# Experts' weights loaded as one consecutive run a partition: a two-layer mixture-of-experts and hybrid mixer kernel

## The chip, the cores and the metric

The kernel is one program on one core of a Trainium2 chip. The metric is the device time of one execution in microseconds (us), as the median of several runs. The core has TensorE (PE; its weight loads are listed apart as PEld), VectorE (DVE), ScalarE (ACT), GpSimd (POOL) and SyncE (SP), which here issues most of the DMAs. All inputs lie in HBM, and all arithmetic data are 32 bits wide.

## What is computed

Two blocks stand one behind the other, each of two layers, for 256 tokens of width 1024 (and 256 context tokens in the first layer). What the change touches is the mixture of experts at the end of each layer of the first block:

```python
D_MODEL = 1024; N_EXPERTS = 32; TOP_K = 2; D_EXPERT = 512; MOE_BLOCK = 128

def hier_moe(h, w_rg, b_rg, w_re, b_re, w1, w3, w2):
    ...                      # a group of 8 experts, then 2 experts of it, for each token
    xs = h[slot_tok].reshape(n_blocks, MOE_BLOCK, d_)
    def run(args):
        xb, e = args
        return (jax.nn.silu(xb @ w1[e]) * (xb @ w3[e])) @ w2[e]
    ys = lax.map(run, (xs, block_e)).reshape(-1, d_)
    return jnp.zeros_like(h).at[slot_tok].add(ys * slot_gate[:, None])
```

`w1` and `w3` of an expert are 1024 x 512 matrices, `w2` is 512 x 1024; each is 2 MB. Layer 0 runs it on 512 tokens (256 of `x` and 256 of `ctx`), layer 1 on 256. Before it, in each layer, stand a modulation, a dense input product, attention, local mixers and a dense output product; behind both layers stands the second block (sliding window and forgetting attention, a state space mixer, memory attention), which has no experts.

## The kernel before

**The stream of weights.** All large weights pass through `Stream`. A unit is a tile `wu` of 128 partitions by 2048 numbers, 1 MB. Units are pushed in the order in which they will be used; `pump` gives the next one a free slot and issues its DMA on SP's queue, where it waits until the last reader of the slot's former content is done. There are some 13 or 14 slots during the experts. `push_kn` (L188) loads the dense weights, `push_ex` (L203) the experts' weights. An expert's number stands in a register that SP reads from the routing result.

**The experts.** The 32 experts are ranked by their load. A plan fixed when the kernel is built gives each rank a capacity of 128 tokens (the first ones; one has 256 in layer 1), 64 or 32, and packs them into groups of 128 rows: one expert of 128 ("b"), two of 64 ("m") or four of 32 ("s"). Blocks of two to four groups are worked through in three stages: A (product with `w1`, silu), B (product with `w3`, multiply), C (transpose of the result, product with `w2`, scatter). A stage of a group takes two halves of the depth, and each half needs one unit of each of the group's experts: two units for a "b" stage, four for "m", eight for "s". A layer has 32 experts of 6 units, 192 units, of which 128 are `w1` or `w3` and 64 are `w2`.

**What a partition of a unit holds.** In `push_ex` the rows of the matrix are split as `(k p)`: partition p holds row k * 128 + p for each k. A unit of `w1` or `w3` has four such rows of 512 numbers (k = 0 to 3), one of `w2` two rows of 1024. So a partition is filled by four runs of 2 KB, or by two of 4 KB.

**What multiplies them.** The rows of a unit are the depth of a product, so the other operand must have its depth on the same partitions. For stages A and B this is `xT`, which `prep` makes one block ahead: `step` (four a block) multiplies the tokens `tok.hi` and `tok.lo` (stationary, 128 columns for each k) by the 0/1 matrix `G` (moving, 128 columns for each group of the block, so 256, 384 or 512), in the rounded 32-bit format. That is `NT` * 2 products for each of 8 k, with `NT` 4 in layer 0 and 2 in layer 1; with 5 blocks a layer, 320 and 160 products. For stage C it is `hT`: `h_` (the tile `sil`, 128 x 512) is transposed by four transposes of 128 columns, 31 groups in all.

**What sets the order.** A scheduler of the tile framework orders each engine's instructions; inside the product loops of stages A, B and C TensorE's order is written by hand (`manual_schedule`), and of a group's experts the last comes first (`last_first`), so that a half starts when its last unit has landed. SP issues in the order of the pushes.

Of the kernel before, what the change touches and what calls it, by code (L numbers as in the profile page):

```python
# [31 lines left out]
P = 128  # L32
# [106 lines left out]
class Stream:  # L139
# [62 lines left out]

    def push_ex(self, src, reg, k0, per, n):  # L203

        def fn(t):
            r = reg()
            self.last = self.nc.sync.dma_start(  # L207
                t[:, :per * n].rearrange("p (k f) -> p k f", k=per),
                src[ds(r, 1), k0 * P:(k0 + per) * P, :].rearrange("o (k p) f -> p (o k) f", p=P)).ins
        self.push(fn, 2)  # L210

    def get_kn(self, ks, n):
# [20 lines left out]
class Kern:  # L233
# [924 lines left out]
    def moe_main(self, l, NT, pl, tok, acc, G2, mp0, end_plan, load_numbers):  # L1158
# [4 lines left out]
        with ExitStack() as es:  # L1163
# [5 lines left out]
            def prep(b):  # L1169

                gb = [groups[g] for g in blocks[b]]
                n = len(gb) * P
                G = T([P, NT, 512], "G", 1, F32R)
                for i, (w, ps_, base) in enumerate(gb):
                    nj, p0 = len(ps_), ps_[0]
                    nc.vector.tensor_tensor(
                        G[:, :, i * P:(i + 1) * P].rearrange("p t (j w) -> p t j w", j=nj),
                        self.iota[:, base:base + w][:, None, None, :].to_broadcast([P, NT, nj, w]),
                        pl["pos"][:, :, p0:p0 + nj][:, :, :, None].to_broadcast([P, NT, nj, w]),
                        op=OP.is_equal)  # L1180
                Gf = G.bitcast(F32)
                xq = []

                def step(q):
                    xt = T([P, 2, 512], "xT", 4)
                    for kk in range(2):
                        k = 2 * q + kk
                        ps = self.pt("t")
                        for t in range(NT):
                            for z, src in enumerate((tok.hi, tok.lo)):  # L1190
                                self.mm(ps[:, :n], src[:, t, k * P:(k + 1) * P], G[:, t, :n],
                                        t == 0 and z == 0, t == NT - 1 and z == 1)
                        self.ev(xt[:, kk, :n], ps[:, :n])
                    xq.append(xt)

                def gates():
                    pgate = self.pt("s")
                    for i, (w, ps_, base) in enumerate(gb):
                        for t in range(NT):
                            for j, p in enumerate(ps_):  # L1200
                                self.mm(pgate[w * j:w * (j + 1), i:i + 1],
                                        Gf[:, t, i * P + w * j:i * P + w * (j + 1)], pl["gs"][:, t, p:p + 1],
                                        t == 0, t == NT - 1)
                    gcol = T([P, 4], "gcol", 2)
                    nc.vector.tensor_copy(gcol[:, :len(gb)], pgate[:, :len(gb)])
                    return gcol
                return dict(xq=xq, step=step, gates=gates)

            def rows(g):
# [53 lines left out]
            for si, (b, z, g) in enumerate(stages):  # L1263
# [9 lines left out]
                if z in "AB":  # L1273
                    ps = self.pt("mm")
# [33 lines left out]
                h_ = sil.pop(g)  # L1308
                tp = self.pt("t")
                for f in range(4):  # L1310
                    self.tr(tp[:, f * P:(f + 1) * P], h_[:, f * P:(f + 1) * P])
                hT = T([P, 4, P], "hT", 2)
                self.ev(hT.rearrange("p f s -> p (f s)"), tp)
                if not any(zz == "B" and bb == b for bb, zz, _ in stages[si:]) and b + 1 < len(blocks):
# [852 lines left out]
```

## Time and profile before

| | us |
|---|---|
| median of 3 runs | 2375.89 (2375.29 to 2379.04) |
| the profiled execution, its own time | 2375.62 |
| its span, first to last instruction | 2374.0 |
| TensorE matmuls busy | 2170.5 (91%) |
| VectorE busy | 1004.6 (42%) |
| ScalarE busy | 702.8 (30%) |
| GpSimd busy | 399.9 (17%) |
| moved by DMA | 598.60 MB, mean 252 GB/s |
| experts of layer 0, TensorE's products | 351 to 876 |
| experts of layer 1, TensorE's products | 1120 to 1636 |

Times inside the span are counted from its first instruction. A matmul's duration in the trace holds its latency, and matmuls overlap: the pace of a row of them is read from their starts. A share of DMA over 1 says that an engine had two packets under way at once. The granted clock is the share of TensorE's full speed; it has two levels, 1.2 and 2.4 GHz, so 0.91 over a stretch is a mixture.

### The profile page before, as it was taken

What the parts mean: (1) busy time and instruction counts of PE and PEld (TensorE: products, weight loads), DVE (VectorE), ACT (ScalarE), POOL (GpSimd) and SP (SyncE); (2) the same over time, 40 slices, a digit from 0 to 9 for tenths busy, and PEclk for the clock granted to TensorE, in tenths of its full rate; (3) what the DMA queues carried; (4) which work ended last, traced back from release to release, by engine and by line L of the source; (5) the groups of instructions that cost most, each with busy time, mean ns of one, the idle gap of its engine ahead of it and who ended that gap; (6) DMA issues with size and microseconds to landing.
All of it is one profiled execution on the core that took longest, in us unless ns stands there. A gap on an engine that the chain in (4) does not pass through costs nothing.

```text
span 2374.0 us, 32289 instructions
## 1 busy us (share of the span) xinstructions
PE 2170.5 (91%) x12723; PEld 1390.7 (59%) x12723; DVE 1004.6 (42%) x1963; ACT 702.8 (30%) x1267; POOL 399.9 (17%) x377
## 2 busy tenths in 40 slices
PE   7999979999998998998888887979999899999898
PEld 4565454443443436656333232325989799998797
DVE  3562562223131447624202212214566665565664
ACT  3344110010010114431110000002568464557653
POOL 0000221214051543012101202112100200100211
PEclk9998969999999998999889888989999899999999
DMA  9444569999999986464999999998444244443341
GB/s 311 137 132 167 200 215 345 387 351 334 400 391 385 401 319 220 156 216 170 342 337 384 384 400 387 400 386 293 152 143 138 91 164 142 143 155 113 107 142 46
DMA packets 330764, 598.60 MB, mean 252 GB/s; under 512 B 22218, under 2 KB 132330, under 8 KB 330604
## 3 DMA queue, kind: packets, MB, share of 16 engines
q1 hardware_dynamic: 322782, 579.22, 67.7%
q0 software_dynamic: 3728, 13.17, 1.6%
q10 hardware_dynamic: 4094, 4.05, 0.5%
q8 instruction: 103, 1.69, 0.3%
q14 instruction: 57, 0.47, 0.1%
HBM read 595.30 MB, written 1.10 MB: 251 GB/s over the span
## 4 chain that ended last, share of the span: by engine, by line
PE 36%; DMA 9%; issue 4%; DVE 2%; ACT 1%; SPq 1%; POOL 0%; DVEq 0%; ACTq 0%; POOLq 0%
PE psmm L276 31%; DMA wu<-in_w_dram 8%; PE pss L276 4%; PE pst L276 1%; PE pst L314 1%; SPq L207 1%; ACT wsplit L289 1%; DVE wsplit L293 1%; DVE yg L1231 0%; DMA c<-in_cst_dram 0%; DVE xd L1881 0%; DVE cvy L1863 0%; POOL mixA1l L293 0%; ACT dM L1922 0%; ACT yh L1339 0%
## 5 line engine op out<-in xcount | busy, mean ns | idle before, releaser
L276 PE MATMUL psmm<-wu,xT 128*32 128x512 f32 (+2 forms) x2080 | 480.4, 654 | 82.6 <-DMA wu<-in_w_dram 72.7
L276 PEld LDWEIGHTS psmm<-wu,xT 128*32 128x32 f32 (+2 forms) x2080 | 157.4, 144 | 370.0 <-issue 277.3
L1233 POOL TENSOR_TENSOR xs<-xs,yg 128x512 f32<-128x512 f32 x120 | 151.9, 1282 | 700.2 <-DVE yg L1231 699.6
L276 PE MATMUL psmm<-h2Th,wsplit 128*128 128x256 f32 x1344 | 258.1, 288 | 4.7 <-ACT zg L1850 3.7
L276 PE MATMUL psmm<-wu,hT 128*32 128x512 f32 (+2 forms) x1040 | 233.9, 633 | 17.0 <-DMA wu<-in_w_dram 16.9
L293 DVE TENSOR_TENSOR wsplit<-wu,wsplit 128x2048 fp32r<-128x2048 f32 x86 | 198.6, 2311 | 60.9 <-ACT wsplit L289 60.1
L276 PEld LDWEIGHTS psmm<-h2Th,wsplit 128*128 128x128 f32 x1344 | 212.9, 191 | 8.4 <-ACT zg L1850 3.9
L1231 DVE TENSOR_TENSOR yg<-pss,G 128x512 f32<-128x512 f32 x176 | 116.8, 687 | 231.5 <-PE pss L276 224.3
L289 ACT CAST wsplit<-wu 128x2048 fp32r<-128x2048 f32 x86 | 163.6, 1902 | 109.5 <-PE psmm L276 77.0
L276 PE MATMUL psmm<-h2Tl,wsplit 128*128 128x256 f32 x672 | 192.5, 287 | 0.0
L276 PEld LDWEIGHTS psmm<-wu,hT 128*32 128x32 f32 (+2 forms) x1040 | 76.4, 139 | 145.6 <-issue 123.5
L1289 DVE TENSOR_TENSOR sil<-sil,psmm 128x512 f32<-128x512 f32 x31 | 21.3, 687 | 317.6 <-PE psmm L276 317.6
L1339 ACT ACTIVATE yh<-psmm,gcol 128x512 fp32r<-128x512 f32 x62 | 41.8, 687 | 295.8 <-PE psmm L276 172.1
L276 PEld LDWEIGHTS psmm<-h2Tl,wsplit 128*128 128x128 f32 x672 | 128.5, 191 | 1.1 <-issue 0.7
L1287 ACT ACTIVATE sil<-psmm 128x512 f32<-128x512 f32 x31 | 18.5, 598 | 275.6 <-PE psmm L276 275.6
L276 PE MATMUL pss<-yh,S 128*128 128x512 f32 x176 | 86.1, 489 | 11.2 <-DVE yg L1231 9.9
L259 ACT COPY xT<-pst 128x512 f32<-128x512 f32 (+2 forms) x36 | 17.8, 497 | 247.7 <-PE psmm L276 146.1
L276 PE MATMUL psmm<-wu,mixT 128*128 128x512 f32 x192 | 90.4, 623 | 0.0
L1341 DVE SCALAR_TENSOR_TENSOR yl<-psmm,gcol,yh 128x512 fp32r<-128x512 f32 x62 | 45.9, 747 | 94.3 <-ACT yh L1339 93.2
L1233 POOL TENSOR_TENSOR cs<-cs,yg 128x512 f32<-128x512 f32 x62 | 77.9, 1278 | 46.1 <-DVE yg L1231 46.1
L519 DVE TENSOR_REDUCE mx<-psmm 128x1 f32<-128x256 f32 (+2 forms) x128 | 53.5, 452 | 50.0 <-PE psmm L276 49.8
L276 PEld LDWEIGHTS pss<-yh,S 128*128 128x128 f32 x176 | 33.1, 188 | 66.7 <-issue 33.5
(582 smaller groups left out, 3966.8 us busy)
## 6 DMA issues: line engine op xcount, KB each, us to landing
wu<-in_w_dram SPq DMA_DIRECT2D x384, 1024.0 KB
wu<-in_w_in_dram SPq DMA_DIRECT2D x62, 1024.0 KB
wu<-in_w_ada_dram SPq DMA_DIRECT2D x48, 1024.0 KB
wu<-in_w_out_dram SPq DMA_DIRECT2D x24, 1024.0 KB
wu<-in_w_mv_dram SPq DMA_DIRECT2D x8, 1024.0 KB
wu<-in_w_mq_dram SPq DMA_DIRECT2D x8, 1024.0 KB
wu<-in_w_mo_dram SPq DMA_DIRECT2D x8, 1024.0 KB
wu<-in_w_mk_dram POOLq DMA_DIRECT2D x4, 1024.0 KB, 12.1
```

The costliest lines, as they stand in the source:

```text
L207: self.last = self.nc.sync.dma_start(t[:, :per * n].rearrange("p (k f) -> p k f", k=per), src[ds(r, 1), k0 * P:(k0 + per) * P, :].rearrang ...
L276: return self.nc.tensor.matmul(out, lhsT, rhs, start=start, stop=stop).ins
L289: self.nc.scalar.copy(out.hi, src)
L293: e.tensor_tensor(out.lo, src, out.hi.bitcast(F32), op=OP.subtract)
L314: self.nc.tensor.transpose(out, in_, self.ident[0:n, 0:n])
L519: nc.vector.reduce_max(mx[:, i:i + 1], s[:, :nk], axis=AX.X)
L1231: nc.vector.tensor_tensor(y, ps, G2[:, who[t], c], op=OP.mult)
L1233: e.tensor_tensor(acc[t][:, c], acc[t][:, c], y, op=OP.add)
L1287: nc.scalar.activation(sil[g], ps, AF.Silu)
L1289: nc.vector.tensor_tensor(sil[g], sil[g], ps, op=OP.mult)
L1339: nc.scalar.activation(a_, yps[h], AF.Copy, scale=gc)
L1341: nc.vector.scalar_tensor_tensor(b_, yps[h], gc, a_.bitcast(F32), op0=OP.mult, op1=OP.subtract)
```

## The change

`push_ex` splits the rows of a block of weights as `(p k)`: partition p of a unit holds rows 4p to 4p + 3 of `w1` or `w3` (2p and 2p + 1 of `w2`), which lie behind each other in HBM, 8 KB in one run. The depth that a partition stands for changes with it, and so do the columns that make `xT` and `hT`: for row k of a unit the tokens' columns o, o + 4, o + 8 ... (128 of them, 16 bytes apart) instead of 128 neighbours, and for the transposes of `sil` every second column (8 bytes apart). Those are the stationary operands of 480 products and of 124 transposes.

```diff
     def push_ex(self, src, reg, k0, per, n):
...
-                src[ds(r, 1), k0 * P:(k0 + per) * P, :].rearrange("o (k p) f -> p (o k) f", p=P)).ins
+                src[ds(r, 1), k0 * P:(k0 + per) * P, :].rearrange("o (p k) f -> p (o k) f", p=P)).ins
...
                         ps = self.pt("t")
+                        o = k // 4 * 512 + k % 4
                         for t in range(NT):
                             for z, src in enumerate((tok.hi, tok.lo)):
-                                self.mm(ps[:, :n], src[:, t, k * P:(k + 1) * P], G[:, t, :n],
+                                self.mm(ps[:, :n], src[:, t, o:o + 4 * P - 3:4], G[:, t, :n],
                                         t == 0 and z == 0, t == NT - 1 and z == 1)
...
                 for f in range(4):
-                    self.tr(tp[:, f * P:(f + 1) * P], h_[:, f * P:(f + 1) * P])
+                    o = f // 2 * 256 + f % 2
+                    self.tr(tp[:, f * P:(f + 1) * P], h_[:, o:o + 2 * P - 1:2])
```

In the built program every engine's instructions stand in the same order before and after, with the same waits. 384 DMAs differ in both operands (before 128 x 4 x 512 or 128 x 2 x 1024, now 128 x 2048), and 604 instructions of TensorE in the stationary one. No instruction is added or taken away.

## Rows read from the trace of the kernel before

**Rows 1.** The page's chain that ended last, shares of the span by line.
```profile
PE psmm L276 31%; DMA wu<-in_w_dram 8%; PE pss L276 4%; PE pst L276 1%; PE pst L314 1%; SPq L207 1%; ACT wsplit L289 1%; DVE wsplit L293 1%; DVE yg L1231 0%; DMA c<-in_cst_dram 0%; DVE xd L1881 0%; DVE cvy L1863 0%; POOL mixA1l L293 0%; ACT dM L1922 0%; ACT yh L1339 0%
```

**Rows 2.** Windows: layer 0's experts, layer 1's, and stretches within each.
```profile
core 0: us, PE busy (x) PEld busy (x) DVE busy (x) ACT busy (x) POOL busy (x), PEclk, DMA share, GB/s
366.00:880.00 514.00, 488.43 (x2305) 214.97 (x2303) 144.87 (x225) 44.62 (x74) 153.25 (x137) 0.98 1.01 379
500.00:546.00 46.00, 44.74 (x192) 21.41 (x191) 16.80 (x26) 4.98 (x8) 20.23 (x18) 1.00 0.78 274
546.00:752.00 206.00, 191.87 (x970) 80.40 (x968) 56.06 (x86) 14.88 (x24) 61.92 (x56) 0.98 1.04 387
1127.00:1640.00 513.00, 426.96 (x2003) 168.52 (x2002) 94.43 (x159) 50.02 (x78) 72.49 (x71) 0.91 1.01 376
1126.00:1258.00 132.00, 108.76 (x525) 44.30 (x523) 19.61 (x37) 18.21 (x25) 11.71 (x14) 0.90 0.92 332
1258.00:1626.00 368.00, 305.69 (x1427) 118.56 (x1431) 70.44 (x115) 29.14 (x49) 57.76 (x53) 0.91 1.04 394
```

**Rows 3.** Waits of PE, windows 366:546, 546:775, 1127:1640, 1258:1626: us, times, longest.
```profile
PE psmm L276 <- DMA wu<-in_w_dram: 3.0, 2, 2.0
PE psmm L276 <- DMA wu<-in_w_dram: 11.5, 5, 5.2
PE psmm L276 <- DMA wu<-in_w_dram: 75.1, 19, 7.2
PE psmm L276 <- DMA wu<-in_w_dram: 53.5, 14, 7.2
```

**Rows 4.** Waits of SP's queue, window 500:546.
```profile
SPq L207 <- PE psmm L276: 39.7, 7, 8.7
```

**Rows 5.** Windows in which `w1` and `w3` alone are loaded, then `w2` alone.
```profile
569.00:591.00 22.00, 21.18 (x92) 7.83 (x90) 5.99 (x9) 1.20 (x2) 9.49 (x10) 1.00 1.05 387
1345.00:1365.00 20.00, 11.05 (x54) 2.58 (x50) 0.00 (x0) 0.60 (x1) 0.00 (x0) 0.74 1.05 387
619.00:638.00 19.00, 18.27 (x100) 9.29 (x96) 2.72 (x4) 2.30 (x4) 0.00 (x0) 1.00 1.03 409
1602.00:1620.00 18.00, 17.66 (x59) 7.87 (x60) 4.93 (x8) 1.85 (x3) 2.71 (x3) 1.00 1.03 409
```

**Rows 6.** The page's DMA packets.
```profile
DMA packets 330764, 598.60 MB, mean 252 GB/s; under 512 B 22218, under 2 KB 132330, under 8 KB 330604
```

**Rows 7.** Tiles `tok0h`, `tok1h`, `sil`: duration ns min/median/max, first and last start, forms.
```profile
L276 PE MATMUL pst<-G,tok0h x160: 276/393/801, 331.6 to 790.2; 128*128 128x512 f32 x96, 128*128 128x256 f32 x64
L276 PEld LDWEIGHTS pst<-G,tok0h x160: 186/188/331, 331.6 to 790.1; 128*128 128x128 f32 x160
L276 PE MATMUL pst<-G,tok1h x80: 282/398/796, 1095.2 to 1513.4; 128*128 128x384 f32 x48, 128*128 128x256 f32 x16, 128*128 128x512 f32 x16
L314 PEld LDWEIGHTS pst<-cst_a_sb,sil x124: 138/140/144, 378.2 to 1615.1; 128*128 128x128 f32 x124
```

**Rows 8.** Timeline of PE and PEld: start us, us; the gather at 512, 256 and 384 columns.
```profile
396.90 0.39 PE L276 MATMUL pst<-G,tok0h 128*128 128x512 f32 x1
397.14 0.39 PE L276 MATMUL pst<-G,tok0l 128*128 128x512 f32 x1
...
338.15 0.33 PEld L276 LDWEIGHTS pst<-G,tok0l 128*128 128x128 f32 x1
338.36 0.33 PEld L276 LDWEIGHTS pst<-G,tok0h 128*128 128x128 f32 x1
...
343.83 0.19 PEld L276 LDWEIGHTS pst<-G,tok0l 128*128 128x128 f32 x1
343.94 0.19 PEld L276 LDWEIGHTS pst<-G,tok0h 128*128 128x128 f32 x1
...
351.29 11.07 PE L276 MATMUL psmm<-wu,xT 128*128 128x512 f32 x22 [6.39 <-PEq L1352]
...
1272.01 0.34 PE L276 MATMUL pst<-G,tok1h 128*128 128x384 f32 x1
1272.19 0.34 PE L276 MATMUL pst<-G,tok1l 128*128 128x384 f32 x1
```

## The prediction

> **What bounds the kernel now.** First I read the chain that ended last: TensorE's products hold the largest part of it, and the one DMA that matters is that of the experts' weights, 8% of the span [rows 1]. So the change is worth what those waits are worth in the two stretches of the experts, and the windows of these were read next. In layer 1 (1127 to 1640) PE waits 75.1 us for experts' units [rows 3] and the DMA engines' share is over 1 on the mean; from 1258 to 1626 it is 1.04 at 394 GB/s [rows 2]. There the transfers set the pace without a break: PE's waits only fill what they leave, and a shorter transfer shortens the stretch. Layer 0 is another case: from 366 to 880 PE is busy for 488 of 514 us [rows 2] and waits 3.0 + 11.5 us for units [rows 3]. Between 500 and 546 the DMAs fall to a share of 0.78 [rows 2], because SP waits 39.7 of those 46 us until PE gives a slot free [rows 4]. So layer 0 is bound by PE but for some 15 us. The rest of the program loads nothing by the changed lines.
>
> **The rate of a run's length** can be read from the same trace. Where `w1` and `w3` alone come in (runs of 2 KB), the rate is 387 GB/s; where `w2` comes in (4 KB), 409 [rows 5], with the engines saturated in both. A unit of 1,048,576 bytes so takes 2.709 us with 512 runs and 2.564 with 256: 256 runs fewer save 0.145 us. If the price of a run is a constant, 128 runs of 8 KB save another 0.073: an estimated 2.491 us, 421 GB/s. No row shows a load of such a run: all but 160 of 330764 packets are shorter than 8 KB [rows 6]. The bounds are 409 GB/s (an 8 KB run is no better than two of 4 KB, or is cut into such) and a run that costs nothing, 2.564 - 0.145 = 2.419 us or 433 GB/s. I take 421: two lengths, in both layers, lie on one line, and 8 KB is one doubling on.
>
> The Trainium skill (DMA: Bandwidth & Descriptors, "Why small descriptors are slow (HBM only)") gives a packet a fixed 3 cycles beside one for each 32 bytes. That would be 67/64 against 131/128, 2.2% between 2 and 4 KB; the rows show 5.7%, so the trace disagrees in size. By the page's figure 8 KB would be 3.4% shorter than 2 KB, and the gain below would be about half of what I take.
>
> **Layer 1.** From 1258 to 1626, 368 us at 394 GB/s are 145 MB; at 421 GB/s they take 344.4 us: **23.6 us less**. PE waits 53.5 us there [rows 3], so it has more than twice that to give before it becomes the bound. From 1126 to 1258 the rate is only 332 GB/s at a share of 0.92 [rows 2]: 43.8 MB or 42 units, with transfers that partly wait for slots. All units on the path would give 42 x (2.66 - 2.49) = 7 us, with 2.66 the mean of two 2.709 and one 2.564; I take 6 (bounds 2 and 7). Layer 1 together: **30 us**.
>
> **Layer 0.** The first 3.0 us of waits stand at the start, where slots come free late and the last four units are on the path: 4 x (2.709 - 2.491) = 0.9 us. The 11.5 us [rows 3] fall behind 546. From 546 to 752 the engines are saturated at 387 GB/s over 206 us [rows 2]; at 421 that stretch could be 206 x (1 - 387/421) = 16.6 us shorter, more than PE waits, so all of the 11.5 go and PE is late next. Layer 0: **12.4 us**. A granted clock of 0.98 there says that some 4% of the 514 us ran at 1.2 GHz [rows 2]; part of that lies behind the waits and may come back, up to 5 us that I leave out of the sum.
>
> **What the strided weight loads cost.** 480 gathers read their stationary operand 16 bytes apart, 124 transposes 8 bytes apart. No row shows such a load with many columns, so it is bounded. It can't be cheaper than neighbours. In layer 0 the gathers at 512 columns go at 0.24 us a piece, while warm loads of 128 columns follow each other at 0.11 [rows 8]: a load twice as long is still hidden under the product. At 384 columns the pace is 0.18 [rows 8], but these stand in layer 1, under PE's waits. At 256 columns there is no cover: load and product are both at 0.11 us. These are 64 products for layer 0's first block, 64 for its last and 32 for layer 1's first [rows 7]; the first blocks' stand ahead of a branch of 6.39 us [rows 8], which comes behind them and hides nothing. The nearest row for what the read can deliver is the transposes' own load: 128 columns of `sil` take 138 ns where a plain load of 128 takes 188 [rows 7], so the same port can deliver faster than a plain load asks, and a slower read has room. I take **0 us**. The other end is a load twice as long: warm 86 x 0.11 = 9.5 us in layer 0, and for the loads at 1.2 GHz (0.21 apart [rows 8]; some 42 in layer 0's start, from 331.6 to 340.5, and some 26 in layer 1's) as much again for each, 42 x 0.21 = 8.8 and 26 x 0.21 = 5.5: 24 us in all, or 10 if only the warm ones grow. The transposes at two elements a line I leave at nothing; doubled, they would cost 124 x 0.055 = 7 us at most, part of it under layer 1's waits.
>
> No instruction is added or moved, so no wait is new: SP issues the same 384 DMAs in the same order, and units of the layers behind, in the same queue, can only come earlier.
>
> **The sum** is made against the profiled execution's own 2375.62 us (span 2374.0), which is within 0.3 us of the median of 2375.89: 2375.6 - 30 - 12.4 = **2333 us**.
>
> **The rivals.**
> *Strided loads cost.* With a load twice as long the gain is 42.4 - (10 to 24): 2343 to 2357, middle 2350. For it speaks that nothing in the trace reads so; against it the fast loads of the transposes. The Trainium skill (SBUF — State Buffer, "Door 1: The DMA port swizzle", the note on cachelines) speaks against this change: lines of 16 bytes, and at least two hits in each are wanted to hide the access. With 32-bit data every gather column would be a line by itself, the transposes would keep two hits; no run here shows it for TensorE. Chance 0.20.
>
> *8 KB is worth no more than 4 KB.* At 409 GB/s layer 1 gives 368 x (1 - 394/409) = 13.5 and 42 x (2.66 - 2.564) = 4, layer 0 up to 206 x (1 - 387/409) = 11, of which some 9 meet a wait: 26 us, 2349. Chance 0.13.
>
> *Slower: the strided load becomes TensorE's bound.* Its place is layer 0, where PE has no waits to give. A load four times as long (0.45 us) would set the pace of the 192 gathers at 512 columns there, 192 x (0.45 - 0.24) = 40 us, the 86 warm ones at 256 columns 86 x 0.34 = 29, the cold ones 68 x 0.24 = 16; the rest lies under layer 1's remaining 45 us of waits. 85 - 42 = 43 us slower, 2418. It turns at about three times, 0.34 us: 19 + 20 + 9 = 48. Nothing in the trace points to so much. Chance 0.06.
>
> *It doesn't do what it says:* the rate belongs to the tensors and not to the runs, and stays 387 and 409; then 2374 to 2377. Against it: the same two rates in both layers [rows 5]. Chance 0.05.
>
> **How the numbers follow.** 0.56 for the forecast (2318 to 2342 with its bounds: the cold clock's 5 us and a rate near 433 on one side, the small costs on the other), 0.20, 0.13, 0.06 and 0.05 for the rivals. A range of 2319 to 2356 holds the first, nearly all of the second and the third; it leaves out the two last and a little at the ends, under 0.2. About 0.2%, 4.8 us, is what can be told from no change. Faster by more than that: the first three cases less a tail, 0.88; within it 0.05; slower 0.07.
>
> **What would show it.** DMA packets of 8 KB, some 49,000 in place of 164,000. In saturated stretches of either kind of weight one rate near 421 GB/s; 409 is the second rival, 387 the last. PE's waits for experts' units near 0 to 3 us in layer 0 and near 45 in layer 1, whose span from its first product to its last shrinks from 516 us by about 30. The gather's loads still at 188 ns and its products 0.24 and 0.11 us apart; a first rival shows as a pace near 0.21 at 256 columns. I am wrong if the rate rises and layer 1 doesn't shrink, or if layer 0's products take longer.

## The result

The changed kernel takes 2342.73 us as the median of 4 runs (2339.2 to 2347.23), beside 2377.47 for the kernel before (2375.29 to 2381.23): a ratio of 0.9853 with a 95% interval of 0.9828 to 0.9879, so 35 us less (29 to 41). The forecast was 2333 in a range of 2319 to 2356: the right sign, and 10 us too much gain. Two later comparisons of the same pair gave ratios of 0.9887 and 0.9875 (below). The profiled execution took 2339.62 us, span 2338.0.

The page's chain by line, and the page's packets:

```profile
PE psmm L277 30%; DMA wu<-in_w_dram 8%; PE pss L277 4%; PE pst L277 2%; PE pst L315 1%; ACT wsplit L290 1%; DVE wsplit L294 1%; DVE yg L1233 0%; DVE cvy L1866 0%; DVE xd L1884 0%; SPq L208 0%; POOL mixA1l L294 0%; ACT dM L1925 0%; ACT yh L1342 0%; ACT cvy L1864 0%
DMA packets 216076, 598.60 MB, mean 256 GB/s; under 512 B 22218, under 2 KB 132330, under 8 KB 166764
```

216076 - 166764 = 49,312 packets are now not under 8 KB, 160 before [rows 6], and there are 114,688 fewer in all for the same megabytes. The change does what it says. The chain still holds 8% of experts' transfers, but `pst L277`, the gather, went from 1% to 2% [rows 1]: the first sign of what the change cost.

Windows of the kernel after: layer 0's experts, three stretches of it, layer 1's saturated stretch, and two stretches in which before only `w1` and `w3`, or only `w2`, came in. The last columns are the granted clock, the DMA engines' share and GB/s.

```profile
core 0: us, PE busy (x) PEld busy (x) DVE busy (x) ACT busy (x) POOL busy (x), PEclk, DMA share, GB/s
366.00:876.00 510.00, 495.85 (x2307) 235.37 (x2306) 144.04 (x224) 44.16 (x74) 152.75 (x136) 0.99 0.94 379
500.00:546.00 46.00, 44.75 (x190) 23.34 (x189) 16.32 (x26) 4.98 (x8) 20.21 (x18) 1.00 0.65 249
546.00:743.00 197.00, 190.82 (x958) 85.99 (x960) 55.70 (x86) 14.88 (x24) 61.94 (x56) 0.98 0.98 405
569.00:591.00 22.00, 21.19 (x104) 7.70 (x106) 6.00 (x9) 1.20 (x2) 9.50 (x10) 1.00 1.01 421
619.00:638.00 19.00, 18.10 (x112) 9.32 (x111) 2.21 (x4) 1.96 (x4) 0.00 (x0) 1.00 1.02 422
1258.00:1590.00 332.00, 296.86 (x1386) 124.70 (x1380) 69.37 (x114) 29.19 (x49) 56.91 (x53) 0.94 1.00 413
```

Both kinds of weights now come in at 421 or 422 GB/s, from 387 and 409 [rows 5]. Layer 1's saturated stretch, at 394 before [rows 2], runs at 413. In layer 0 the DMA share fell from 1.01 to 0.94 at the same mean of 379 GB/s [rows 2]: the transfers now wait more for TensorE (SP's queue waits for the experts' products for 352 us there, for 199 before). And PE's busy time there grew from 488 to 496 us in a shorter window.

PE's waits for experts' units in layer 0 (345 to 880) and layer 1 (1110 to 1640): us, times, longest. Then tiles of PEld: duration in ns, minimum, median and maximum; the second row is the last of layer 0's gathers (770 to 790).

```profile
PE psmm L277 <- DMA wu<-in_w_dram: 3.1, 4, 1.4
...
PE psmm L277 <- DMA wu<-in_w_dram: 45.0, 13, 6.3
```

```profile
L277 PEld LDWEIGHTS pst<-G,tok0h x160: 307/310/335, 330.4 to 786.2; 128*128 128x128 f32 x160
L277 PEld LDWEIGHTS pst<-G,tok0h x8: 309/332/335, 778.9 to 786.2; 128*128 128x128 f32 x8
L315 PEld LDWEIGHTS pst<-cst_a_sb,sil x124: 193/207/223, 378.6 to 1583.4; 128*128 128x128 f32 x124
```

The waits fell from 14.5 to 3.1 us in layer 0 and from 75.1 to 45.0 in layer 1 [rows 3], as forecast. The loads are the news: a gather's takes 310 ns (188 before), a transpose's 207 (138) [rows 7].

The products show what that adds up to. Rows of the first and last product of each layer's experts (the two numbers behind the durations are first and last start), first in the kernel after, then in the kernel before the last row of layer 0 and both of layer 1:

```profile
L277 PE MATMUL psmm<-wu,xT x1024: 591/592/1202, 352.8 to 853.7; 128*64 128x512 f32 x70, 128*32 128x512 f32 x65, 128*128 128x512 f32 x36
L277 PE MATMUL psmm<-wu,hT x512: 590/592/697, 387.7 to 871.5; 128*64 128x512 f32 x77, 128*32 128x512 f32 x63, 128*128 128x512 f32 x31
L277 PE MATMUL psmm<-wu,xT x1056: 591/593/1116, 1116.6 to 1575.4; 128*32 128x512 f32 x106, 128*128 128x512 f32 x38, 128*64 128x512 f32 x32
L277 PE MATMUL psmm<-wu,hT x528: 591/592/1062, 1149.6 to 1603.2; 128*32 128x512 f32 x105, 128*128 128x512 f32 x39, 128*64 128x512 f32 x32
```

```profile
L276 PE MATMUL psmm<-wu,hT x512: 590/592/1062, 389.0 to 875.0; 128*64 128x512 f32 x77, 128*32 128x512 f32 x63, 128*128 128x512 f32 x31
...
L276 PE MATMUL psmm<-wu,xT x1056: 591/593/1115, 1120.1 to 1607.1; 128*32 128x512 f32 x106, 128*128 128x512 f32 x38, 128*64 128x512 f32 x32
L276 PE MATMUL psmm<-wu,hT x528: 592/592/1063, 1160.7 to 1635.3; 128*32 128x512 f32 x105, 128*128 128x512 f32 x39, 128*64 128x512 f32 x32
```

Layer 1 goes from its first product at 1116.6 to the end of its last at 1603.7: 487.1 us, 515.7 before. Layer 0, from its first gather at 330.4 [the tile row above] to 872.1, takes 541.7; before it took 544.0 (331.6 [rows 7] to 875.6). So of the 12 us expected in layer 0 this profile shows 2, and the two later ones of the same kernel show none.

### The profile page after: what moved, and what is told of

Read it like the earlier page. It is cut to its first block, busy times and chain, and to the rows that moved or that the text cites. A ratio compares the mean times of both kernels' runs of the same rounds, so it can differ in the third digit from the quotient of the medians.

```text
span 2338.0 us, 32289 instructions
## 1 busy us (share of the span) xinstructions
PE 2179.5 (93%) x12723; PEld 1426.4 (61%) x12723; DVE 1003.5 (43%) x1963; ACT 702.7 (30%) x1267; POOL 399.8 (17%) x377
## 2 busy tenths in 40 slices
DMA packets 216076, 598.60 MB, mean 256 GB/s; under 512 B 22218, under 2 KB 132330, under 8 KB 166764
## 4 chain that ended last, share of the span: by engine, by line
PE 36%; DMA 8%; issue 4%; DVE 2%; ACT 2%; POOL 0%; SPq 0%; DVEq 0%; ACTq 0%; POOLq 0%
PE psmm L277 30%; DMA wu<-in_w_dram 8%; PE pss L277 4%; PE pst L277 2%; PE pst L315 1%; ACT wsplit L290 1%; DVE wsplit L294 1%; DVE yg L1233 0%; DVE cvy L1866 0%; DVE xd L1884 0%; SPq L208 0%; POOL mixA1l L294 0%; ACT dM L1925 0%; ACT yh L1342 0%; ACT cvy L1864 0%
## 5 line engine op out<-in xcount | busy, mean ns | idle before, releaser
L277 PE MATMUL psmm<-wu,xT 128*32 128x512 f32 (+2 forms) x2080 | 476.6, 647 | 47.5 <-DMA wu<-in_w_dram 39.8
L277 PEld LDWEIGHTS psmm<-wu,xT 128*32 128x32 f32 (+2 forms) x2080 | 158.2, 142 | 329.0 <-issue 278.7
L277 PE MATMUL psmm<-h2Th,wsplit 128*128 128x256 f32 x1344 | 257.2, 288 | 4.7 <-ACT zg L1853 3.7
L277 PE MATMUL psmm<-wu,hT 128*32 128x512 f32 (+2 forms) x1040 | 226.9, 604 | 8.3 <-DMA wu<-in_w_dram 8.2
L277 PEld LDWEIGHTS psmm<-h2Th,wsplit 128*128 128x128 f32 x1344 | 212.0, 190 | 8.4 <-ACT zg L1853 3.9
L277 PE MATMUL psmm<-h2Tl,wsplit 128*128 128x256 f32 x672 | 191.7, 286 | 0.0
L277 PEld LDWEIGHTS psmm<-wu,hT 128*32 128x32 f32 (+2 forms) x1040 | 75.3, 135 | 130.1 <-issue 116.8
L277 PEld LDWEIGHTS psmm<-h2Tl,wsplit 128*128 128x128 f32 x672 | 127.9, 190 | 1.0 <-issue 0.7
L277 PE MATMUL pss<-yh,S 128*128 128x512 f32 x176 | 86.5, 491 | 10.9 <-DVE yg L1233 9.8
L277 PE MATMUL psmm<-wu,mixT 128*128 128x512 f32 x192 | 89.8, 619 | 0.0
L1344 DVE SCALAR_TENSOR_TENSOR yl<-psmm,gcol,yh 128x512 fp32r<-128x512 f32 x62 | 45.9, 746 | 78.5 <-ACT yh L1342 77.4
L277 PEld LDWEIGHTS pss<-yh,S 128*128 128x128 f32 x176 | 33.4, 190 | 66.0 <-issue 33.1
## 6 DMA issues: line engine op xcount, KB each, us to landing
wu<-in_w_mk_dram POOLq DMA_DIRECT2D x4, 1024.0 KB, 12.4
```

What stands on the lines that cost most here:

```text
L277: return self.nc.tensor.matmul(out, lhsT, rhs, start=start, stop=stop).ins
L1344: nc.vector.scalar_tensor_tensor(b_, yps[h], gc, a_.bitcast(F32), op0=OP.mult, op1=OP.subtract)
```

## The experiments

Each profile below is cut into the same five stages, read from the first gather, the first product with `xT` and the last with `hT` of each layer. The time ahead of layer 0's gather and that behind layer 1 wander by some 5 us between profiles of kernels that are equal there, so the verdicts go by the two layers. A ratio stands against runs of before on the same chip in the same comparison, whose medians were 2374 to 2377. All in us.

| kernel | median | ratio to before, 95% | ahead of layer 0's gather | layer 0, gather to last product | up to layer 1's first product | layer 1, first to last product | behind |
|---|---|---|---|---|---|---|---|
| before | 2375.89 | | 331.6 | 544.0 | 244.5 | 515.7 | 738.2 |
| after | 2342.73 | 0.9828 to 0.9879 | 330.4 | 541.7 | 244.5 | 487.1 | 734.3 |
| after_again | 2346.49 | 0.9871 to 0.9904 | 332.1 | 545.1 | 244.7 | 486.2 | 735.3 |
| after_third | 2347.29 | 0.9853 to 0.9898 | 333.1 | 545.2 | 245.5 | 486.6 | 738.0 |
| plain_loads | 2329.03 | 0.9787 to 0.9824 | 331.9 | 531.9 | 244.6 | 483.6 | 738.6 |
| strided_only | 2387.34 | 1.0046 to 1.0080 | 333.7 | 554.1 | 245.8 | 514.2 | 737.0 |
| tokens_permuted | 2338.24 | 0.9814 to 0.9866 | 339.0 | 531.9 | 246.3 | 485.9 | 736.9 |
| w2_short_runs | 2392.68 | 1.0045 to 1.0092 | 330.4 | 550.1 | 244.4 | 529.1 | 737.9 |
| w2_long_runs | 2370.4 | 0.9965 to 0.9989 | 331.1 | 545.9 | 242.7 | 512.2 | 735.2 |
| tokens_written_permuted | 2348.92 | 0.9868 to 0.9908 | 335.3 | 534.5 | 252.0 | 486.4 | 735.4 |
| other_steps | 2341.74 (one run) | | 335.2 | 533.4 | 245.4 | 487.5 | 738.6 |
| steps_by_layer | 2334.63 | 0.9807 to 0.9853 | 332.0 | 533.9 | 244.8 | 484.6 | 734.0 |
| two_in_both | 2340.86 | 0.9830 to 0.9874 | 330.6 | 536.8 | 244.2 | 491.3 | 735.6 |

Profiles of equal kernels differ in layer 0 by up to 3.5 us (541.7 to 545.2 for the kernel after), and most of that is the granted clock. Added up over layer 0, the stretches granted at 1.2 GHz are 28.6 us long in the first of those three profiles and 35.6 and 33.3 in the others. The gathers of neighbours go at 0.21 us a piece at that level and at 0.11 at the other [rows 8], so I estimate that half of such time is lost: 3.5 and 2.3 us more than in the first profile, of the 3.4 and 3.5 measured. In the profile of the kernel before these stretches are 32.7 us long.

The theory after the result: the transfers gave what was forecast, and the strided loads of TensorE took some 10 us of it back in layer 0. The rival: the loads are free, and the transfers gave less. "Warm" stands below for a granted clock of 2.4 GHz, "cold" for 1.2.

**The transfers alone.** The loads read neighbours, the DMAs are those of after:

```diff
-                                self.mm(ps[:, :n], src[:, t, o:o + 4 * P - 3:4], G[:, t, :n],
+                                self.mm(ps[:, :n], src[:, t, k * P:(k + 1) * P], G[:, t, :n],
...
-                    self.tr(tp[:, f * P:(f + 1) * P], h_[:, o:o + 2 * P - 1:2])
+                    self.tr(tp[:, f * P:(f + 1) * P], h_[:, f * P:(f + 1) * P])
```

> The changed kernel's DMAs, but the gathers and the transposes read neighbouring columns again, as before the change. The rows of the weights then don't meet the right columns: which depth is multiplied with which is changed, the amount of work and its order are not. Theory (the strided weight loads took back part of the gain, in layer 0 where TensorE is the bound): the gathers at 256 columns go back from 0.235 us a piece to 0.11 to 0.12, which is 64 x 0.12 = 7.7 us for layer 0's last block and about 3 us for the two first blocks; 2342.7 - 10 = about 2332 us, with layer 0 (first gather to last product) at 532 instead of 542 and layer 1 at 486 to 488 as it is. Rival (layer 0 gave little because something else of TensorE's work there took the place of the waits): within 2 us of the changed kernel, 2340 to 2345.

2329.03 us (2324.84 to 2332.82) where the kernel after took 2346.49 beside it. Layer 0 is 12.1 us shorter than before, and PE is left with these waits for experts' units there:

```profile
PE psmm L277 <- DMA wu<-in_w_dram: 4.4, 3, 2.4
```

The forecast was 12.4. The waits fell by 10.1 us, from 14.5 to 4.4, where 11.5 and 0.9 were to go; another 1.6 are the estimate for 29.5 us at 1.2 GHz in place of 32.7. The whole is 17 us under the kernel after, where about 10 were expected: 13.2 of them lie in layer 0, and 2.6 in layer 1, where none was expected. The theory holds.

**The loads alone.** The DMAs of before, the columns of after (the same edit on the other side):

```diff
-                                self.mm(ps[:, :n], src[:, t, k * P:(k + 1) * P], G[:, t, :n],
+                                self.mm(ps[:, :n], src[:, t, o:o + 4 * P - 3:4], G[:, t, :n],
...
-                    self.tr(tp[:, f * P:(f + 1) * P], h_[:, f * P:(f + 1) * P])
+                    self.tr(tp[:, f * P:(f + 1) * P], h_[:, o:o + 2 * P - 1:2])
```

> The kernel before, with the strided columns of the gathers and transposes but its old runs of 2 and 4 KB (so the depths don't meet: what is multiplied with what is changed, not the amount). Theory: only the cost of the strided loads is left. In layer 0 about 3 us at the start and 64 x 0.12 = 7.7 us in the last block, of which part falls into the 5 us of waits for weights behind 752; in layer 1 the transfers hide it. 2377 + 6 to 11 = 2383 to 2388 us. Rival (strided loads are covered everywhere): 2376 to 2379.

2387.34 us, slower than before by 0.46 to 0.80%. Layer 0 takes 10.1 us more, layer 1 none (514.2 against 515.7): there the loads lie under the waits for transfers. In layer 0 the 10.1 are a balance: the waits for experts' units fell from 14.5 to 8.5 us, so part of the loads' cost lies under them, and 42.3 us at 1.2 GHz in place of 32.7 added an estimated 4.8. A stretch of `w1` and `w3` in it still has the old rate, at the last column:

```profile
569.00:591.00 22.00, 21.66 (x81) 9.03 (x81) 6.54 (x12) 1.20 (x2) 6.91 (x6) 0.92 1.05 387
```

**The reordering elsewhere.** The DMAs of after; the tokens' columns are put in the new order when they are split into `tok.hi` and `tok.lo`, so that ScalarE and VectorE read every fourth number and the gathers read neighbours:

```diff
-            self.split(tok[:, t, c], hx[:, c])
+            v = lambda z: z[:, t, c].rearrange("p (k q) -> p k q", k=4)
+            self.split(Pair(v(tok.hi), v(tok.lo)), hx[:, c].rearrange("p (q k) -> p k q", k=4))
...
-                                self.mm(ps[:, :n], src[:, t, o:o + 4 * P - 3:4], G[:, t, :n],
+                                self.mm(ps[:, :n], src[:, t, k * P:(k + 1) * P], G[:, t, :n],
...
```

> The changed kernel with the tokens written in the order in which the gather wants them: ScalarE and VectorE read the modulated tokens with a step of 16 bytes when they make the high and low parts (24 pairs of instructions), and the gather's loads are plain. The transposes of sil stay strided. Theory: the gathers' cost goes, 8 to 10 us, and the strided reads of ScalarE and VectorE cost at most their own length again (24 x 0.6 us on each, part of it on the path to the first gather), so 2333 to 2340 us; at best equal to the kernel with plain loads. Rival (the loads are not what layer 0 lacks): 2341 to 2350.

2338.24 us (2330.18 to 2343.19). Layer 0 has its 531.9 us again, with the transposes still 8 bytes apart: those cost nothing that can be seen (layer 0 has 26.4 us at 1.2 GHz here, 29.5 with plain loads, which could hide an estimated 1.6). The split pays instead. ScalarE's copy in this kernel, then in the kernel after, and VectorE's subtraction likewise:

```profile
L290 ACT CAST tok0h<-hx x8: 1113/1134/1169, 279.0 to 318.5; 128x512 fp32r<-128x512 f32 x8
```

```profile
L290 ACT CAST tok0h<-hx x8: 613/618/619, 273.3 to 310.4; 128x512 fp32r<-128x512 f32 x8
```

```profile
L294 DVE TENSOR_TENSOR tok0l<-hx,tok0h x8: 1044/1492/3728, 280.1 to 322.6; 128x512 fp32r<-128x512 f32 x8
```

```profile
L294 DVE TENSOR_TENSOR tok0l<-hx,tok0h x8: 677/814/3424, 274.0 to 314.2; 128x512 fp32r<-128x512 f32 x8
```

From the first copy to the first gather there are 339.0 - 279.0 = 60.0 us, 330.4 - 273.3 = 57.1 in the kernel after, and in layer 1 29.0 beside 25.7: 3 us a layer paid for some 10 in layer 0.

**The kernel after once more**, beside these three:

> The changed kernel once more beside the others: 2339 to 2347 us, layer 0 from its first gather to its last product about 542 us and layer 1 from its first expert product 487 us. What differs between this profile and the first one is the noise of a stage: both theories expect under 2 us in the experts' stages.

2346.49 us (2344.22 to 2349.59), ratio 0.9887: 28 us under before. Layer 0's 545.1 us are what before takes, and 3.4 more than in the first profile, where under 2 were expected of the noise.

**The price of a run, or of a tensor?** Both kinds of weights changed at once, so `w2` was changed alone, in both directions. In shorter runs first, its half rows one behind the other (the products read them where they lie):

```diff
+            s = src[ds(r, 1), k0 * P:(k0 + per) * P, :]
+            if n == 1024:
+                self.last = self.nc.sync.dma_start(
+                    t.rearrange("p (h k f) -> p h k f", h=2, k=per),
+                    s.rearrange("o (k p) (h f) -> p h (o k) f", p=P, h=2)).ins
...
-                                        u[j][0][:, (k % 2) * 1024 + h * 512:(k % 2) * 1024 + (h + 1) * 512],
+                                        u[j][0][:, h * 1024 + (k % 2) * 512:h * 1024 + (k % 2 + 1) * 512],
```

> The kernel before with w2 alone loaded another way: its tile is filled half row by half row, so each partition takes four runs of 2 KB in place of two of 4 KB, and the products read the same numbers from where they now lie. Theory (the price belongs to the run, some 9 ns of a DMA engine each): the stretches of w2 fall from 409 to 387 GB/s, the rate of w1 and w3; layer 1 gets 54 units x 0.145 = 8 us longer, layer 0 0 to 4 us, so 8 to 12 us more than the kernel before beside it, about 2384. Rival (the rate belongs to the tensor: w2's place in HBM or its readers): w2 stays at 409 and the time within 3 us of before.

2392.68 us: 16 us more, where 8 to 12 were expected. A stretch of `w2` in this kernel:

```profile
615.00:640.00 25.00, 22.58 (x114) 10.79 (x112) 3.45 (x5) 2.35 (x4) 0.00 (x0) 1.00 1.05 387
```

`w2` in runs of 2 KB has the rate of `w1` and `w3`; the price belongs to the run. Layer 1 got 13.4 us longer where 8 were expected, with PE's waits up by 10.0 (75.1 to 85.1). Layer 0 got 6.1 us longer where 0 to 4 were expected, with its waits as they were (14.6 us, 14.5 before). The granted clock fits both remainders: layer 0 has 45.7 us at 1.2 GHz in place of 32.7, layer 1 102.4 in place of 95.6, an estimated 6.5 us and up to 3.4 (some of layer 1's lies under waits). Whether the edit or chance lowered the clock is not shown. Then `w2` alone in runs of 8 KB:

```diff
-                src[ds(r, 1), k0 * P:(k0 + per) * P, :].rearrange("o (k p) f -> p (o k) f", p=P)).ins
+                src[ds(r, 1), k0 * P:(k0 + per) * P, :].rearrange("o (p k) f -> p (o k) f" if n == 1024 else "o (k p) f -> p (o k) f", p=P)).ins
...
+                    o = f // 2 * 256 + f % 2
-                    self.tr(tp[:, f * P:(f + 1) * P], h_[:, f * P:(f + 1) * P])
+                    self.tr(tp[:, f * P:(f + 1) * P], h_[:, o:o + 2 * P - 1:2])
```

> The kernel before with w2 alone changed: 8 KB runs and transposes of every second column; w1, w3 and the gathers as before. Theory: w2 at 421 GB/s, w1 and w3 still at 387, layer 1 54 units x 0.073 = 4 us shorter, layer 0 0 to 2 us shorter, the transposes' loads at 207 ns and for nothing, so 3 to 6 us less than before, 2369 to 2373. Rival (the transposes' longer loads cost too, 124 x 0.069 = 8.6 us, half of it in layer 0): 2375 to 2380.

2370.4 us, faster than before by 0.11 to 0.35%. Windows of `w2` and of `w1` with `w3`:

```profile
619.00:638.00 19.00, 18.32 (x100) 9.42 (x97) 2.76 (x4) 2.35 (x4) 0.00 (x0) 1.00 1.02 422
...
569.00:591.00 22.00, 21.18 (x87) 7.88 (x89) 5.99 (x9) 1.20 (x2) 10.10 (x10) 1.00 1.05 386
```

One tensor at 422 beside another at 386 in the same run, and layer 1 is 3.5 us shorter (4 expected). With the transposes 8 bytes apart here too, 1.9 us more in layer 0 is within what profiles differ by (36.4 us at 1.2 GHz, 32.7 before: an estimated 1.9).

**What a load pays by.** The kernel after with the gathers' columns 8 bytes apart in layer 0 and 32 in layer 1:

```diff
-                        o = k // 4 * 512 + k % 4
+                        m = 8 if l else 2
+                        o = k // m * (m * P) + k % m
...
-                                self.mm(ps[:, :n], src[:, t, o:o + 4 * P - 3:4], G[:, t, :n],
+                                self.mm(ps[:, :n], src[:, t, o:o + m * P - m + 1:m], G[:, t, :n],
```

> The kernel after with the gathers' columns 8 bytes apart in layer 0 and 32 bytes apart in layer 1 (the tokens' columns then do not belong to the weights' rows, so the mixture's result is another one). Theory (a load pays for the 16-byte lines that it touches, one each from 16 bytes on): at 32 bytes the pace of the gathers stays at 0.235 us, at 8 bytes it is near half way, 0.16 to 0.17 at 256 columns, and layer 0 gets 5 to 7 us shorter than after, some 2336. Rival 1 (two hits in a line hide the access): 0.11 to 0.12 at 8 bytes, layer 0 some 10 us shorter. Rival 2 (the load pays by the step itself): 0.45 us at 32 bytes, layer 1 up to 10 us longer.

The loads of layer 0, then of layer 1 in this kernel:

```profile
L277 PEld LDWEIGHTS pst<-G,tok0h x160: 193/195/330, 335.2 to 781.3; 128*128 128x128 f32 x160
```

```profile
L277 PEld LDWEIGHTS pst<-G,tok1h x80: 312/335/345, 1088.0 to 1489.9; 128*128 128x128 f32 x80
```

At 8 bytes 195 ns (188 for neighbours), and the median pace from start to start at 256 columns is 0.122 us (0.119 before): free, and layer 0 is at 533.4. My theory of a price half way, 0.16, was wrong, and the first rival right. At 32 bytes the pace at 384 columns is 0.245 us, 0.235 at 16 bytes: the second rival, 0.45, is wrong. If the read goes by lines of 16 bytes, as the theory has it, one number in a line costs a doubling, two in a line cost nothing, and empty lines between matter little. The whole time of this kernel rests on one run; what it shows are the paces and layer 0.

**The reordering one step earlier.** The addition that makes the tokens puts them in the new order, and the split reads neighbours. The edit's writes are not 16 bytes apart, as the expectation says: of four numbers behind each other each goes 128 positions, 512 bytes, behind the last:

```diff
-            e.tensor_tensor(hx[:, c], z[:, c], A[:, c], op=OP.mult)
-            e.tensor_tensor(hx[:, c], hx[:, c], B[:, c], op=OP.add)
+            y = dp.tile([P, 512], F32, name=self.nm("res"), tag="res", bufs=2)
+            e.tensor_tensor(y, z[:, c], A[:, c], op=OP.mult)
+            v = lambda z: z.rearrange("p (q k) -> p q k", k=4)
+            e.tensor_tensor(hx[:, c].rearrange("p (k q) -> p q k", k=4), v(y), v(B[:, c]), op=OP.add)
...
```

> The kernel after, with the tokens' columns put into the order of the depth where they are made: the addition that ends the modulation writes every fourth position (16 bytes apart) into its output, the split that follows and the gathers read neighbours, and the scatter's reader takes them back. Theory: the gathers' 10 us in layer 0 come back and the writes 16 bytes apart cost little, since four additions a layer carry them: 2328 to 2334, as fast as the loads of neighbours alone made it. Rival (a write 16 bytes apart is as slow as the read was for VectorE and ScalarE, about half a microsecond more for each of 8 to 12 operations ahead of the gather): 2334 to 2340.

2348.92 us (2345.24 to 2351.77): a miss on both sides, no better than the kernel after. Layer 0 is short again (534.5), but the stretch between the layers grew to 252.0 from 244.5 and the one ahead of layer 0's gather by 3 us. VectorE's addition, at least 678 ns in the kernel after, now takes at least 1034:

```profile
L928 DVE TENSOR_TENSOR hx<-res,B x8: 1034/1980/3052, 272.9 to 1074.9; 128x512 f32<-128x512 f32 x8
```

Its input also shares the two buffers of the residual's tile, which can hold work up; the two causes were not told apart. A write 16 bytes apart was not run.

**A kernel from what was learnt.** Layer 0, which TensorE bounds, takes two runs of 4 KB for `w1` and `w3` and gathers 8 bytes apart; layer 1, which the transfers bound, keeps 8 KB and 16 bytes. Beside it the same in both layers, and the kernel after:

```diff
-                t[:, :per * n].rearrange("p (k f) -> p k f", k=per),
-                src[ds(r, 1), k0 * P:(k0 + per) * P, :].rearrange("o (p k) f -> p (o k) f", p=P)).ins
+                t[:, :per * n].rearrange("p (h k f) -> p h (k f)", k=j, f=n),
+                src[ds(r, 1), k0 * P:(k0 + per) * P, :].rearrange("o (h p k) f -> p (o h) (k f)", p=P, k=j)).ins
...
-                    self.ws.push_ex(self.a[src][l], reg(p), k0, per, n)
+                    self.ws.push_ex(self.a[src][l], reg(p), k0, per, n, per if l else 2)
...
-                        o = k // 4 * 512 + k % 4
+                        m = 4 if l else 2
+                        o = k // m * (m * P) + k % m
...
-                                self.mm(ps[:, :n], src[:, t, o:o + 4 * P - 3:4], G[:, t, :n],
+                                self.mm(ps[:, :n], src[:, t, o:o + m * P - m + 1:m], G[:, t, :n],
```

> The kernel after with layer 0's w1 and w3 in two runs of 4 KB a partition (rows 2p and 2p + 1 of each half of a unit) and so the gathers' columns 8 bytes apart there; w2 and all of layer 1 as after, 8 KB and 16 bytes. Theory (a load of TensorE at two numbers of a 16-byte line is as fast as neighbours, one a line takes twice as long; layer 0 is bound by TensorE and needs the rate only for its 11.5 us of waits): the gathers at 256 columns back to 0.12 us, w1 and w3 there at 409 GB/s, which still meets some 9 of the 11.5 us; layer 0 from its first gather to its last product 533 to 536 us (after: 542 to 545), layer 1 unchanged at 486 to 487; 7 to 10 us less than the kernel after beside it. Rival (layer 0 needs the 421 GB/s too): it gains under 3 us.

> The same in both layers: w1 and w3 in runs of 4 KB, gathers 8 bytes apart, w2 in runs of 8 KB. Theory: layer 0 as in the run by layer, 533 to 536 us; layer 1, bound by the transfers, loses 0.073 us for each of the about 105 units of w1 and w3 on its path, 7 to 8 us: 494 to 495 from its first product to its last; in all within 3 us of the kernel after. Rival (the gathers' strided loads cost layer 1 too): layer 1 loses under 4 us and the kernel is faster than after by over 4.

> The kernel after, unchanged, beside the two above: 2340 to 2347, layer 0 from its first gather to its last product 542 to 545 us, layer 1 from its first product to its last 486 to 487.

By layer: 2334.63 us (2330.95 to 2342.32), 13 us under the kernel after beside it (2347.29), where 7 to 10 were expected, and 41 under before. Layer 0 takes 533.9 us against 545.2, as expected; layer 1, which is the same in both kernels, takes 2.0 us less. Its windows (layer 0 behind 546, then `w1` and `w3` in each layer) and loads:

```profile
546.00:743.00 197.00, 186.54 (x960) 80.44 (x952) 54.93 (x84) 14.88 (x24) 60.36 (x53) 0.99 1.01 407
569.00:591.00 22.00, 21.19 (x110) 7.58 (x112) 5.99 (x9) 1.20 (x2) 9.26 (x9) 1.00 1.02 402
...
1345.00:1365.00 20.00, 20.00 (x82) 8.51 (x76) 2.02 (x4) 1.06 (x2) 0.00 (x0) 0.86 1.01 420
```

```profile
L276 PEld LDWEIGHTS pst<-G,tok0h x160: 193/195/331, 332.0 to 778.7; 128*128 128x128 f32 x160
L276 PEld LDWEIGHTS pst<-G,tok1h x80: 307/314/335, 1084.7 to 1484.0; 128*128 128x128 f32 x80
```

Layer 0 needs the rate only for its waits, and 402 to 407 GB/s nearly covers them (PE still waits 5.5 us there). The 402 is no rate of a run: the window holds a dip (410 GB/s from 569 to 580, 394 from 580 to 591). With 4 KB in both layers, `w1` and `w3` in layer 1 come in at 409, as `w2` did before at that length:

```profile
1437.00:1456.00 19.00, 7.63 (x46) 1.71 (x46) 0.00 (x0) 0.60 (x1) 0.00 (x0) 0.80 1.03 409
```

Layer 1 then takes 491.3 us where the two others have 484.6 and 486.6: 5 to 7 us lost (7 to 8 expected), and PE waits 56.2 us for experts' units there, 47.7 and 49.0 in the others. The whole, 2340.86, was a miss: it was expected within 3 us of the kernel after and is 6.4 under it, because 8.4 us of layer 0 (536.8 against 545.2) outweigh what layer 1 lost. That total is what the rival said, but not for its reason of a loss under 4 us in layer 1. By the layers, layer 1 is better served by runs of 8 KB and layer 0 by gathers 8 bytes apart; the kernel by layer has both.

## Why the prediction was right, and where it was not

**The bound: right.** Layer 1 gave the gain, because its transfers set the pace; layer 0 had 14.5 us to give and no more.

**The rate: right to the number.** 421 GB/s from a line through two points, 387 and 409; measured 421 and 422, in `w2` alone as in both. That "two lengths lie on one line" was no evidence, as any two points do; the third length is the first test of a constant price a run, and it passed. By the Trainium skill's 3 cycles a packet (DMA: Bandwidth & Descriptors, "Why small descriptors are slow (HBM only)") 8 KB would take an estimated 3.4% less time than 2 KB. The rows give 387/421, 8.1% less, so the measurement decides against the page's size.

**Layer 1: right.** 30 us forecast; 28.6, 29.5 and 29.1 in three profiles of the kernel after, with waits of 45.0 (45.9 and 49.0 in the later two) where "near 45" was said. The two terms of the sum can be told apart, since the products stand in the same order in both kernels, and there luck helped. The product that ends the first wait behind 1258, at 1262.15 before, stands 142.1 us behind the layer's first product; after, at 1250.93, it stands 134.3 behind it, so 7.8 us came ahead of it (9.2 and 8.0 in the later profiles) where 6 was taken and 7 was the bound. Behind it 20 to 21 us came, not 23.6: the stretch ran at a mean of 413 GB/s and not at 421 throughout. One term's excess made up for the other's lack.

**Layer 0's transfers: right.** 12.4 forecast, 12.1 when the loads read neighbours, of which 10.1 are waits. The clock's "up to 5 us", left out of the sum, rightly stayed out: layer 0 has a mean of 32.5 us at 1.2 GHz in the three profiles of the kernel after, 32.7 before.

**What the strided weight loads cost: the step that failed.** I took 0 between bounds of 0 and 24. It is 10 to 13 us, as far as can be told all in layer 0: 10.1 from the loads alone (the balance above), 544.0 (the mean of 541.7, 545.1 and 545.2) less 531.9 = 12.1 from taking them away, 545.2 - 533.9 = 11.3 from steps of 8 bytes. Its parts, by the median pace: the last block's 64 products at 256 columns went from 0.119 to 0.234 us, 7.4 us; the first block up to the first product, 22.4 to 22.9 us where 19.7 were, 3 us; the 192 at 512 columns from 0.234 to 0.238, 1 us. These 11.4 are what the waits gave, 14.5 less about 3, and so layer 0 stood still. So the warm products doubled and the cold ones hardly moved, and that was the lower of the two costs I had worked out (10). These are loads of the first block in the kernel after, at a granted clock of 0.50 (331 to 339) and, near its end, of 1.00 (346 to 349):

```profile
332.04 0.33 PEld L277 LDWEIGHTS pst<-G,tok0l 128*128 128x128 f32 x1
332.27 0.33 PEld L277 LDWEIGHTS pst<-G,tok0h 128*128 128x128 f32 x1
...
346.08 0.33 PEld L277 LDWEIGHTS pst<-G,tok0l 128*128 128x128 f32 x1
346.32 0.33 PEld L277 LDWEIGHTS pst<-G,tok0h 128*128 128x128 f32 x1
...
352.81 1.19 PE L277 MATMUL psmm<-wu,xT 128*128 128x512 f32 x1 [4.32 <-PEq L1355]
```

They stand 0.23 us apart in both places; before they stood 0.21 apart cold and 0.11 warm [rows 8]. The reason I gave for 0 was the fast load of the transposes, "the same port can deliver faster than a plain load asks". But those rows read neighbours, and say nothing of a read that uses one number in a line. The note that I quoted against the change, the Trainium skill's SBUF — State Buffer ("Door 1: The DMA port swizzle", on cachelines of 16 bytes and two hits), is what the runs bear out, on both its sides: 310 ns at one number a line, 195 at two. I gave it 0.20; a stated rule with no row against it deserved more than an inference from rows of another access.

"Hides nothing", I said of the branch behind the first block: it hid a little. Its wait went from 6.39 [rows 8] to 4.32 us while the block's gathers grew.

**The rivals.** *Strided loads cost* is what happened, at its low end: 2343 worked out, 2342.73 measured; with 2346.49 and 2347.29 in the later comparisons, agreement to the microsecond is luck. It was not an alternative to the forecast but the forecast with one term right. *8 KB worth no more than 4 KB* is out by the 421. The slower one asked for a load three times as long; it is twice. *The rate belongs to the tensors* fell with `w2` at 387 in 2 KB runs and `w1` and `w3` at 409 in 4 KB runs.

**Open.** Layer 1 with plain loads took 483.6 us against 486 to 487, but 484.6 with strided ones in the kernel by layer; whether the loads cost anything there can't be told. Its time at 1.2 GHz differs as much: 61.4 us with plain loads, 64.9 to 68.3 in the kernel after, 58.0 in the kernel by layer.

## What to carry to other kernels

The rate of a saturated transfer could here be extrapolated from two run lengths in the same trace, and it is worth its full size only in the stage whose waits the transfers end. A layout that makes runs longer hands its stride to whoever reads the other operand: with 32-bit numbers, 8 bytes apart cost TensorE's loads nothing here and 16 bytes doubled a warm one, so keep the step at 8, and take 16 only where the reader has waits to hide it. Before a few microseconds between two profiles are explained, compare how long each was granted the lower clock. Choose the layout by stage if the bounds differ.

## What the runs showed of the hardware

- Transfers into 128 partitions, engines saturated: 387 GB/s with runs of 2 KB, 409 with 4 KB, 420 to 422 with 8 KB, whichever tensor it is.
- A TensorE load of 128 columns of 32 bits, 16 bytes apart, lets products follow each other at 0.233 to 0.235 us at either level of the granted clock; neighbours give 0.21 at 1.2 GHz and 0.11 to 0.12 at 2.4. At 8 bytes it is 0.12 (warm), at 32 bytes 0.245.
- A transpose's load at 8 bytes is recorded at 207 ns instead of 138, while the median pace of the transposes went only from 0.109 to 0.12 us: a load's duration is not its price.
- ScalarE and VectorE pay for reading with a step of 16 bytes too: for 512 columns ScalarE's copy went from a median of 618 ns to 1134, VectorE's subtraction from at least 677 to at least 1044. VectorE's addition that writes with jumps of 512 bytes took at least 1034 ns, 678 before.
- The granted clock moves a stage by microseconds between profiles of one kernel: in layer 0, 28.6 and 35.6 us at 1.2 GHz went with 541.7 and 545.1 us.
